# Third-FFN first chunk split in two parts, and the experts'-end operands moved out of the weight ring

## The chip, the cores and the metric

One core of one Trainium2 chip runs the kernel. The metric is device time in microseconds (us) of one execution. TensorE (PE) multiplies, ScalarE (ACT) and VectorE (DVE) work on tiles, SyncE (SP) issues the transfers; GpSimd (POOL) has nothing to do here.

## What is computed

A transformer block with a mixture of experts and then two layers of a second block, for 256 tokens of width 1024, all in float32. Each of the two layers is FFN, token mixer, FFN, every one of them behind an adaptive norm whose gain, shift and gate come from a product of a condition vector with a large matrix `w_ada`. The parts that the change touches:

```python
def ada_norm(x, g, shift, scale):
    return rms_norm_2(x, g) * (1 + scale[:, None, :]) + shift[:, None, :]

def swiglu(h, w13, w2):
    a, b = jnp.split(h @ w13, 2, axis=-1)
    return (jax.nn.silu(a) * b) @ w2
...
x = first_block(x, ...)            # ends with the experts
for l in range(2):
    h = ada_norm(x, norm_g[l, 0], mod[:, 0, 0], mod[:, 0, 1])
    x = x + 0.5 * mod[:, 0, 2][:, None, :] * swiglu(h, ffn_w13[l, 0], ffn_w2[l, 0])
    ...                            # token mixer, then a second FFN
```

So there are four FFNs: first (layer 0, right behind the experts), second, third (layer 1, right behind the second), fourth.

## The kernel before

**Tiles and products.** The stream `XT` lies transposed, 8 chunks of 128 features by 256 tokens. Weights come from HBM in pieces of 1 MB (128 rows of 2048 floats). A piece lands in a tile of the ring `raw` and is split for PE into a rounded part `hi` and the rest `lo` (`split`, lines 316 and 320): ACT copies 128x1024 to `hi`, DVE subtracts twice 128x512 for `lo`, two such halves to a piece. PE then makes a product of three float32r terms (hi x hi, hi x lo, lo x hi: lines 340 and 342). A product of plain float32 operands needs no split; PE runs it in two passes.

**An FFN's start.** The norm's factor r (one number per token) needs the whole stream. So the first chunk (j = 0) of `w13` is multiplied with x times g, which needs no r: `early` writes x times g into `self.xg` (with two columns of the shift behind the 256 tokens), chunk by chunk as the stream gets ready; `ff_early` (line 617) multiplies it with piece 0 in float32; `ff_joined` applies r afterwards. Meanwhile `rstd` makes r, and `normalize` (lines 533, 378, 379) makes `hl`, the normalized hi and lo, from which the chunks j = 1 to 21 are multiplied (`ff_in`). `xg` and piece 0 both lie in tiles of the ring `raw`. At the end of the experts `xg` is written by DVE (line 544), elsewhere by ACT (line 546).

**Rings.** `rings(raw, split)` closes the three pools `raw`, `hi`, `lo` and opens them anew with other numbers of buffers. The experts run with (6, 3), the FFNs with (4, 5). In the kernel before, `moe_end` switches them, and `ffn` calls it behind `ff_early` and `rstd`. The tiles of a new pool may be written once the old pools that lay in the same place are done with. The same `moe_end` closes the experts' pools `moe0` and `moe1`, opens the ring `ada_pool(2)` for `w_ada` (tiles `araw`), and loads some constants.

**Where the pools lie.** In a partition of SBUF, in bytes: `moe0` from 72,320, `moe1` from 118,240 to 152,608, in it the tile `xl` (the low part of the gathered rows, read by the first-round experts) from 123,840 to 140,224; the first FFN's pool (`hT`, `acc`) from 73,632 to 126,880; the two `araw` tiles behind the experts from 138,976 to 155,360; the (6, 3) rings from 155,232, the (4, 5) rings from 155,360 up to the same end, 229,344; in both the ring `raw` has the upper end.

**Order.** Each engine's order is made when the program is built, by a planner that takes, of the instructions whose inputs its own model holds to be ready, the one that stands first in the code. DVE's subtractions of the second to the sixth half piece behind an FFN's last chunk are tied behind that chunk's square (`HOLD`, `add_sq`, line 462). An `ada` step multiplies one araw tile: the first step behind the experts by eight PE products (line 1089), the steps inside an FFN by four DVE operations (lines 1117 and 1119).

Of the kernel before, what the change touches and what calls it, by code (L numbers as in the profile page):

```python
# [10 lines left out]
F32 = mybir.dt.float32  # L11
F32R = mybir.dt.float32r
# [3 lines left out]
AF = mybir.ActivationFunctionType  # L16
OP = mybir.AluOpType
# [3 lines left out]
P = 128  # L21
S = 256
D = 1024
NC = 8
# [8 lines left out]
RINGS = (4, 5)  # L33
# [191 lines left out]
class Net:  # L225
# [269 lines left out]
    def after(self, ins, prev):  # L495
        self.tc.add_manual_dep(ins.ins, prev.ins.name, mybir.DependencyInfo(
            mybir.DependencyClass.NoSync, mybir.DependencyReason.DATA), reason="activation table")
# [35 lines left out]
            nc.vector.scalar_tensor_tensor(h, self.XT[:, c, :], gs[:, c:c + 1], r, OP.mult, OP.mult)  # L533
            self.put_hl(hl, c, h, None if shift is None else shift[:, c:c + 1])

    def early(self, gs, shift, m, dve=False):

        nc = self.nc
        if m == 0:
            self.xg = self.raw()[:, 0:NC * 258].rearrange("p (a c) -> p a c", a=NC)  # L540
            nc.vector.tensor_copy(self.xg[:, :, 256:258], shift[:, :, None].to_broadcast([P, NC, 2]))
        out, x, g = self.xg[:, m, 0:256], self.XT[:, m, :], gs[:, m:m + 1]
        if dve:
            nc.vector.tensor_scalar(out, x, g, None, OP.mult)
        else:
            nc.scalar.activation(out, x, AF.Copy, scale=g)

    def newton(self, x, n):

# [31 lines left out]
    def out_proj(self, dram, hl, gate=None, after=None, early=None):  # L581
        for j in range(4):
            one = j == 3
            for a, ps in enumerate(self.pair(dram[j], hl, "x", one)):
                m = 2 * j + a
                self.resid(ps, m, gate, one)
                after(m) if after else self.add_sq(m, 2)
                if early:
                    early(m)
# [15 lines left out]
            nc.vector.tensor_tensor(s, s, tb, OP.mult)  # L605
        self.put_hl(hT, j, s)

    def ff_early(self, dram):

        nc = self.nc  # L610
        pss = [self.ps("x"), self.ps("x")]
        raw = self.raw()
        nc.sync.dma_start(raw[:, 0:2048], dram)
        for k in range(NC):
            for a, ps in enumerate(pss):
                o = 256 * k + a * P
                nc.tensor.matmul(ps[:, 0:258], raw[:, o:o + P], self.xg[:, k, :], start=(k == 0), stop=(k == NC - 1))  # L617
        return pss
# [12 lines left out]
    def ff_out(self, hT, dram, gate, after, gs=None):  # L631
        h = NFF // 2
        for m in range(NC):
            ps = self.ps("x")
            one = m == NC - 1
            for a in range(2):
                self.mm_t([ps], self.piece(dram[2 * m + a], h, P), P, P, hT, a * h, a == 0, a == 1, one)
            if one:
                self.ada_flush()
            self.resid(ps, m, gate, one)  # L640
            self.add_sq(m)
            if gs is not None:
                self.early(*gs, m)
            if not one:
                after(m)


    def first_block(self):
        nc = self.nc
        self.table("natural_log_exp_and_others")  # L650

        hl = self.hl()
        g = self.v("mix_g", 0, 8)
        for c in range(NC):
            x = self.XT[:, c, :]
            nc.scalar.activation(hl[:, c, 0, :], x, AF.Copy, scale=g[:, c:c + 1])
            nc.vector.scalar_tensor_tensor(hl[:, c, 1, :], x, g[:, c:c + 1], hl[:, c, 0, :].bitcast(F32), OP.mult, OP.subtract)  # L657
        self.mark("norm1")
        self.ada_pool(2)
        es, T = self.phase("mix1")  # L660
        mix = self.mixer1(hl, T)
        self.table("natural_log_exp_and_others")
        es.close()
        self.m1_es.close()
        self.mark("ada0")
        self.ada(ADA1[0])
        self.mark("out1")
        self.ada_pool(4)
        es, T = self.phase("moe0")
        moe = Moe(self, T)  # L670
        self.out_proj(self.ap["w1o"], mix, after=moe.token_rows)
        self.mark("ada0")
        self.ada(ADA1[1])
        self.ada_pool()
        self.rings(6, 3)
        es2, moe.T = self.phase("moe1")
        moe.run()

        def end():
            es2.close()  # L680
            es.close()
            self.rings(*RINGS)
            self.ada_pool(2)
            self.second_consts()
        self.moe_end = end
# [485 lines left out]
    def ffn(self, l, f, sub, gate, n0, n1, n2, ph=None, nxt=None):  # L1171

        self.mark(f"ffi{l}{f}")
        assert self.ada_at >= 40 * l + (8, 32)[f]
        first = self.ff_early(self.ap[f"w13_{l}{f}"][0])
        r = self.rstd(self.nps[:, :256], 1.0 / D)
        if l == f == 0:
            self.moe_end()
        self.ada(n0)
        es, hT, acc = ph or self.ffn_phase(l, f, n1 + n2)  # L1180
        hl = self.hl()
        self.table("silu_and_others")
        self.normalize(hl, r, *sub)
        self.ff_joined(hT, first, r)
        for j in range(NFF):
            if j:
                self.ff_in(hT, j, self.ap[f"w13_{l}{f}"][j], hl)
            self.ada((j + 1) * n1 // NFF - j * n1 // NFF, acc)
        self.table("natural_log_exp_and_others")
        assert self.ada_at >= (40 * l + 16, 48 if l == 0 else 80)[f]  # L1190
        self.mark(f"ffo{l}{f}")
        self.ff_out(hT, self.ap[f"w2_{l}{f}"], gate, lambda m: self.ada((m + 1) * n2 // 7 - m * n2 // 7, acc), nxt)
        es.close()
# [383 lines left out]
class Moe:  # L1577
# [312 lines left out]
    def run(self):  # L1890
        net, nc, T = self.net, self.net.nc, self.T
# [11 lines left out]
        net.tc.no_sync_barrier()  # L1903
        net.mark("gather")

        xs = (net.t(net.hl_p, [P, NC, 512], F32R, "hl"), T([P, NC, 512], "xl", 1, F32R))
        for c in range(NC):
            for src, dst in zip((hh, hw), xs):
                pg = net.ps("x")
                for t in range(2):  # L1910
                    nc.tensor.matmul(pg, src[:, t, c * P:(c + 1) * P], Pm[:, t, 0:512], start=(t == 0), stop=(t == 1))
                if c % 2 or dst is xs[0]:
                    nc.scalar.activation(dst[:, c, :], pg, AF.Copy)
                else:
                    nc.vector.tensor_copy(dst[:, c, :], pg)
        for t in range(2):
            nc.vector.tensor_tensor(Pm[:, t, 512:].rearrange("p (c n) -> p c n", n=64),
                                    self.iota[:, None, :64].to_broadcast([P, 12, 64]),
# [2 lines left out]
        gs = self.slot_gates(lambda t, g: Pm[:, t, g * P:(g + 1) * P].bitcast(F32), self.TILES)  # L1921
# [14 lines left out]

        net.mark("moe")

        def after(m):
            net.sum_sq(m)  # L1940
            for e in range(2):
                net.early(net.gs[0][:, 0:8], net.mod[0][:, 0:8], m + e, True)


        n = len(self.WORK)
        x, yos = {}, [self.T0([P, 2, 4, 256], "m8", 4, F32R) for _ in range(2)]
        pgs, ys = {}, {}
        for i in range(n + 2):
            if i < n:
                g = self.WORK[i]  # L1950
                r, es = self.TILES[g]
                if r and r not in x:
                    x[r] = gathered(r)
                if r == 0:
                    sl = slice(g * P, (g + 1) * P)
                    pgs[g] = self.split_in(g, lambda c: xs[0][:, c, sl], lambda c: xs[1][:, c, sl])
                else:
                    o = (g % 2) * P
                    pgs[g] = self.whole_in(r, es, lambda c: x[r][:, c, o:o + P])
            if i >= 2:  # L1960
                g = self.WORK[i - 2]
                PT = self.tokens(lambda t: Pm[:, t, g * P:(g + 1) * P])
                if i == n + 1:
                    net.table("natural_log_exp_and_others")
                    net.mark("scat")
                self.scatter(ys.pop(g), PT, "aa" if i < n + 1 else "ddaa", None if i < n + 1 else after)
            if 1 <= i <= n:
                g = self.WORK[i - 1]
                r, es = self.TILES[g]
                y = self.whole_out(r, es, pgs.pop(g), gs[:, g]) if r else self.split_out(g, pgs.pop(g), gs[:, g])  # L1970
                ys[g] = self.rows_out(y, yos[i % 2])
# [64 lines left out]
```

## Time and profile before

| | |
|---|---|
| Median of 3 runs | 1429.32 us (1427.37 to 1429.59) |
| The profiled execution | 1427.89 us, its span 1426.1 us |
| Granted TensorE clock, mean over the span | 0.989 |
| Busy share | PE 96%, DVE 74%, ACT 54% |
| HBM read | 324 MB, 228 GB/s over the span |

Matmul records overlap, so PE's busy share says whether it was waiting, not how well it ran. The kernel's time is the span plus 1.8 us around it.

### The profile page before, as it was taken

Reading aid. Unit: us, or ns where it says so; the run is one execution under the profiler, and the core shown is the slowest. Engines: PE = TensorE matmul, PEld = TensorE weight load, DVE = VectorE, ACT = ScalarE, POOL = GpSimd, SP = SyncE. Lnnn points to the kernel's source line nnn. Section 1 sums busy time; section 2 is a strip of 40 time slices with the busy share of each in tenths; the row PEclk is TensorE's granted clock in tenths of the full one; section 3 lists DMA queues with packets and bytes.
Section 4 is the critical chain, followed back from the end, with each engine's and each line's share of the span. In section 5 each row is a group of like instructions: output and inputs, shape, how many; then the busy total and the mean of one; then the engine's idle time right before and its main releaser. Section 6 shows DMA issues by size and latency. Waiting matters only on the chain.

```text
span 1426.1 us, 21863 instructions
## 1 busy us (share of the span) xinstructions
PE 1369.0 (96%) x8054; PEld 1093.7 (77%) x8059; DVE 1052.3 (74%) x2412; ACT 770.8 (54%) x1483; POOL 0.2 (0%) x4
## 2 busy tenths in 40 slices
PE   7998899998999999898999999999999998999997
PEld 6756575545888888566888888888888676888886
DVE  8997645537988557676999876798688586877664
ACT  7555434324665544544766556565555455766553
POOL 0000000000000000000000000000000000000000
PEclk9999899999999999999999999999999999999999
DMA  8744578885886558632688575887487623455452
GB/s 311 285 162 172 238 269 337 337 330 225 334 318 230 171 170 308 239 131 89 213 306 307 179 265 180 330 310 267 155 300 284 247 94 115 156 202 197 142 180 71
DMA packets 51391, 326.49 MB, mean 229 GB/s; under 512 B 6209, under 2 KB 7378, under 8 KB 18898
## 3 DMA queue, kind: packets, MB, share of 16 engines
q1 hardware_dynamic: 50994, 324.86, 62.0%
q8 instruction: 64, 1.05, 0.3%
q14 instruction: 45, 0.37, 0.1%
q10 hardware_dynamic: 288, 0.20, 0.1%
HBM read 324.00 MB, written 1.05 MB: 228 GB/s over the span
## 4 chain that ended last, share of the span: by engine, by line
PE 88%; DVE 5%; ACT 3%; DMA 2%; issue 1%; SPq 0%; DVEq 0%; ACTq 0%
PE psd L340 13%; PE pse L340 12%; PE psa L340 10%; PE psd L342 7%; PE pse L342 6%; PE psa L342 6%; PE psd L356 3%; PE psd L358 3%; PE psd L357 3%; PE psd L1825 3%; PE psm L1089 2%; PE pse L1825 2%; PE psa L1881 1%; DVE lo L320 1%; PE psd L617 1%
## 5 line engine op out<-in xcount | busy, mean ns | idle before, releaser
L320 DVE TENSOR_TENSOR lo<-raw,hi 128x512 fp32r<-128x512 f32 x832 | 503.6, 628 | 175.9 <-ACT hi L316 174.9
L316 ACT ACTIVATE hi<-raw 128x1024 fp32r<-128x1024 f32 (+3 forms) x418 | 400.6, 962 | 339.3 <-PE pse L340 82.0
L340 PE MATMUL psd<-hl,hi 128*128 128x512 f32 x592 | 213.5, 401 | 9.3 <-DVE hl L657 6.8
L340 PE MATMUL pse<-hl,hi 128*128 128x512 f32 x496 | 177.0, 398 | 5.4 <-ACT hi L316 5.4
L342 PE MATMUL psd<-hl,lo 128*128 128x256 f32 x640 | 180.2, 283 | 0.0
L340 PE MATMUL psa<-hl,hi 128*128 128x512 f32 x464 | 164.3, 395 | 0.8 <-ACT hi L316 0.6
L342 PE MATMUL pse<-hl,lo 128*128 128x256 f32 x512 | 144.0, 281 | 0.0
L342 PE MATMUL psa<-hl,lo 128*128 128x256 f32 x512 | 143.7, 281 | 0.0
L340 PEld LDWEIGHTS psd<-hl,hi 128*128 128x128 f32 x592 | 111.5, 189 | 38.7 <-ACT hi L316 8.6
L342 PEld LDWEIGHTS psd<-hl,lo 128*128 128x128 f32 x640 | 121.8, 190 | 1.2 <-DVE lo L320 0.7
L340 PEld LDWEIGHTS pse<-hl,hi 128*128 128x128 f32 x496 | 93.7, 189 | 29.8 <-ACT hi L316 6.3
L340 PEld LDWEIGHTS psa<-hl,hi 128*128 128x128 f32 x464 | 86.9, 188 | 21.0 <-ACT hi L316 0.9
L342 PEld LDWEIGHTS pse<-hl,lo 128*128 128x128 f32 x512 | 97.3, 190 | 0.5 <-DVE lo L320 0.4
L342 PEld LDWEIGHTS psa<-hl,lo 128*128 128x128 f32 x512 | 96.7, 189 | 0.9 <-DVE lo L320 0.4
L1119 DVE SCALAR_TENSOR_TENSOR acc<-araw,cact,acc 128x512 f32<-128x512 f32 x118 | 85.5, 745 | 0.1
L356 PE MATMUL psd<-hi,hl 128*128 128x512 f32 (+3 forms) x224 | 84.6, 378 | 0.8 <-ACT hl L378 0.4
L357 PE MATMUL psd<-lo,hl 128*128 128x512 f32 (+3 forms) x224 | 83.7, 374 | 0.0
L358 PE MATMUL psd<-hi,hl 128*128 128x512 f32 (+3 forms) x224 | 83.1, 373 | 0.0
L340 PE MATMUL pse<-hT,hi 128*128 128x512 f32 x220 | 78.2, 398 | 0.0
L340 PE MATMUL psd<-hT,hi 128*128 128x512 f32 x220 | 78.0, 397 | 0.0
L342 PE MATMUL pse<-hT,lo 128*128 128x256 f32 x264 | 74.3, 281 | 0.0
L342 PE MATMUL psd<-hT,lo 128*128 128x256 f32 x264 | 74.2, 281 | 0.0
(565 smaller groups left out, 2425.5 us busy)
## 6 DMA issues: line engine op xcount, KB each, us to landing
raw<-w SPq DMA_DIRECT2D x88, 1024.0 KB, 5.0
araw<-wada SPq DMA_DIRECT2D x64, 1024.0 KB, 6.9
raw<-w SPq DMA_DIRECT2D x64, 704.0 KB, 4.1
raw<-egu SPq DMA_DIRECT2D x32, 1024.0 KB, 7.2
raw<-edn SPq DMA_DIRECT2D x16, 1024.0 KB, 6.7
raw<-w2n SPq DMA_DIRECT2D x12, 1024.0 KB, 6.4
raw<-cw SPq DMA_DIRECT2D x8, 1024.0 KB, 6.4
araw<-wadb SPq DMA_DIRECT2D x8, 1024.0 KB, 6.0
```

The lines of the kernel that those rows point to most:

```text
L316: nc.scalar.activation(hi[:, f:g], src[:, f:g], AF.Copy)
L320: ins = nc.vector.tensor_tensor(lo[:, f:g], src[:, f:g], hi[:, f:g].bitcast(F32), OP.subtract)
L340: nc.tensor.matmul(ps[:M, :].rearrange("p (a b) -> p a b", a=2), hi[:, o:o + M], xhl[:, k0 + k, :, :], start=st, stop=False)
L342: nc.tensor.matmul(ps[:M, 0:256], lo[:, o:o + M], xhl[:, k0 + k, 0, :], start=False, stop=sp)
L356: nc.tensor.matmul(o, xh, wh, start=st, stop=False)
L357: nc.tensor.matmul(o, xh, wl, start=False, stop=False)
L358: nc.tensor.matmul(o, xl, wh, start=False, stop=sp)
L617: nc.tensor.matmul(ps[:, 0:258], raw[:, o:o + P], self.xg[:, k, :], start=(k == 0), stop=(k == NC - 1))
L1089: self.together(4, lambda j: self.nc.tensor.matmul(self.ada_acc[32 * j:32 * j + 32, :n], lhsT, rhs[:, n * j:n * j + n], start=start, stop= ...
L1119: nc.vector.scalar_tensor_tensor(acc[:, w], raw[:, w], self.cact[:, c, 0:1], acc[:, w], OP.mult, OP.add)
L1825: self.net.halves(lambda h: nc.tensor.matmul(out[p(h)], lhsT[:, p(h)], rhs(h), start=start, stop=stop, tile_position=(0, 64 * h)))
L1881: nc.tensor.matmul(ps[:, 256 * e:256 * e + 256], y[:, i, m0 + k, e * P:(e + 1) * P], PT, start=(e == 0 and i == 0), stop=(i == 1), skip_gr ...
```

## The change

Two places change.

1. **Behind the experts (first FFN).** `xg` and piece 0 no longer lie in the ring `raw`: both lie in one tile `last` of pool `moe1`, with the tag `xl` (the tag grows by 64 bytes, and `hl` by 128, so that `xl` begins at 123,968 and ends at 140,416; piece 0 is its upper half). The switch of the rings to (4, 5) moves from `moe_end`, behind `ff_early`, to right behind `moe.run()`. The rest of `moe_end` stays where it was. `early` still writes with DVE there.
2. **Third FFN.** `xg` is now a tile of pool `hl`, in two parts (hi by ACT, lo by DVE, per chunk of the second FFN's end). Piece 0 is split like all others, `ff_early` makes three float32r products of 258 columns for each float32 one, and `normalize` writes `hl` into the same tile over `xg`.

The second and the fourth FFN keep the float32 form in the ring `raw`.

```diff
-    def early(self, gs, shift, m, dve=False):
+    def early(self, gs, shift, m, xg=None):
         nc = self.nc
+        x, g = self.XT[:, m, :], gs[:, m:m + 1]
+        sh = shift[:, :, None].to_broadcast([P, NC, 2])
+        if xg == "split":
+            if m == 0:
+                self.xg = self.t(self.hl_p, [P, NC, 2, 258], F32R, "hl")
+                hi = self.xg[:, :, 0, 256:258]
+                nc.scalar.activation(hi, sh, AF.Copy)
+                nc.vector.tensor_tensor(self.xg[:, :, 1, 256:258], sh, hi.bitcast(F32), OP.subtract)
+            hi, lo = (self.xg[:, m, i, 0:256] for i in range(2))
+            nc.scalar.activation(hi, x, AF.Copy, scale=g)
+            nc.vector.scalar_tensor_tensor(lo, x, g, hi.bitcast(F32), OP.mult, OP.subtract)
+            return
         if m == 0:
-            self.xg = self.raw()[:, 0:NC * 258].rearrange("p (a c) -> p a c", a=NC)
+            self.xg = (self.raw() if xg is None else xg)[:, 0:NC * 258].rearrange("p (a c) -> p a c", a=NC)
...
-    def ff_early(self, dram):
+    def ff_early(self, dram, raw=None):
         pss = [self.ps("x"), self.ps("x")]
-        raw = self.raw()
+        if len(self.xg.shape) == 4:
+            pieces = self.piece(dram, NC, 256)
+            for ip, (hi, lo, ks) in enumerate(pieces):
+                for a, ps in enumerate(pss):
+                    for i, k in enumerate(ks):
+                        o = 256 * i + a * P
+                        for j, (w, x) in enumerate(((hi, 0), (hi, 1), (lo, 0))):
+                            nc.tensor.matmul(ps[:, 0:258], w[:, o:o + P], self.xg[:, k, x, :], start=(ip == i == j == 0),
+                                             stop=(ip == len(pieces) - 1 and i == len(ks) - 1 and j == 2))
+            return pss
+        if raw is None:
+            raw = self.raw()
         nc.sync.dma_start(raw[:, 0:2048], dram)
...
         es2, moe.T = self.phase("moe1")
         moe.run()
+        self.rings(*RINGS)
         def end():
             es2.close()
             es.close()
-            self.rings(*RINGS)
             self.ada_pool(2)
             self.second_consts()
...
-        first = self.ff_early(self.ap[f"w13_{l}{f}"][0])
+        first = self.ff_early(self.ap[f"w13_{l}{f}"][0], self.raw0 if l == f == 0 else None)
...
-        hl = self.hl()
+        hl = self.xg[:, :, :, 0:256] if len(self.xg.shape) == 4 else self.hl()
...
+        last = None
         def after(m):
+            nonlocal last
+            if m == 0:
+                last = T([P, NC * 514], "xl")
+                net.raw0 = last[:, NC * 258:]
             net.sum_sq(m)
             for e in range(2):
-                net.early(net.gs[0][:, 0:8], net.mod[0][:, 0:8], m + e, True)
+                net.early(net.gs[0][:, 0:8], net.mod[0][:, 0:8], m + e, last)
```

## Rows read from the trace of the kernel before

**Rows 1.** The page's chain that ended last: its shares by engine.

```profile
PE 88%; DVE 5%; ACT 3%; DMA 2%; issue 1%; SPq 0%; DVEq 0%; ACTq 0%
```

**Rows 2.** Timeline, PE, behind the experts: start us, us, engine line, operation, count, [idle before].

```profile
325.86 3.65 PE L1825 MATMUL pse<-raw,ehf 128*64 128x512 f32 x16
...
336.63 6.26 PE L617 MATMUL psd<-raw,raw 128*128 128x258 f32 x28
342.82 1.06 PE L1089 MATMUL psm<-araw,cact 128*32 128x512 f32 x8
349.29 0.80 PE L340 MATMUL pse<-hl,hi 128*128 128x512 f32 x1 [5.41 <-ACT hi L316]
...
352.77 0.39 PE L340 MATMUL pse<-hl,hi 128*128 128x512 f32 x1
...
353.12 0.39 PE L340 MATMUL pse<-hl,hi 128*128 128x512 f32 x1
```

**Rows 3.** The chain in order of time, same stretch: start us, us, what.

```profile
342.92 4.93 DMA raw<-w
...
348.18 1.06 ACT hi L316
```

**Rows 4.** Waits of the transfer queue (SP), 310 to 346 us: total, times, longest.

```profile
SPq L695 <- DVE m L1857: 13.9, 1, 13.9
SPq L300 <- PE psd L617: 7.0, 1, 7.0
```

**Rows 5.** Windows: busy us of PE, PEld, DVE, ACT, POOL; granted clock, DMA share, GB/s.

```profile
343.00:349.30 6.30, 0.89 (x9) 0.01 (x1) 4.68 (x15) 2.62 (x6) 0.00 (x0) 0.99 0.84 317
349.30:351.00 1.70, 1.70 (x4) 1.17 (x5) 1.70 (x3) 1.57 (x2) 0.00 (x0) 0.50 1.05 443
...
366.60:378.00 11.40, 11.40 (x68) 10.05 (x67) 11.32 (x23) 7.18 (x13) 0.00 (x0) 1.00 0.93 374
```

**Rows 6.** Timeline, PE, from the second FFN's end into the third.

```profile
873.44 0.28 PE L337 MATMUL pse<-hT,hi 128*128 128x256 f32 x1
...
873.67 0.28 PE L342 MATMUL pse<-hT,lo 128*128 128x256 f32 x1
...
882.91 7.13 PE L617 MATMUL psa<-raw,raw 128*128 128x258 f32 x32
889.97 1.92 PE L1089 MATMUL psm<-araw,cact 128*32 128x512 f32 x16
891.83 0.50 PE L340 MATMUL psd<-hl,hi 128*128 128x512 f32 x1
```

**Rows 7.** Timeline, DVE, from the second FFN's end into the third.

```profile
881.92 2.49 DVE L320 TENSOR_TENSOR lo<-raw,hi 128x512 fp32r<-128x512 f32 x4
884.33 1.27 DVE L533 SCALAR_TENSOR_TENSOR w<-XT,gs,w 128x256 f32<-128x256 f32 x3
...
891.51 0.41 DVE L626 TENSOR_TENSOR w<-psa,w 128x256 f32<-128x256 f32 x1
```

**Rows 8.** Timeline, DVE, behind the experts.

```profile
337.79 1.67 DVE L533 SCALAR_TENSOR_TENSOR w<-XT,gs,w 128x256 f32<-128x256 f32 x4 [2.41 <-ACT w L490]
...
339.71 1.67 DVE L379 SCALAR_TENSOR_TENSOR hl<-w,mod,hl 128x256 fp32r<-128x256 f32 x4
...
344.86 0.48 DVE L379 SCALAR_TENSOR_TENSOR hl<-w,mod,hl 128x256 fp32r<-128x256 f32 x1
```

**Rows 9.** Timeline, SP, behind the experts: the issues in their order.

```profile
332.03 0.34 SPq L695 DMA_DIRECT2D k_cmask<-k_cmask  x1
...
335.38 0.43 SPq L1106 DMA_DIRECT2D araw<-wada  x1
...
342.92 2.12 SPq L300 DMA_DIRECT2D raw<-w  x4
```

**Rows 10.** The tile araw, 300 to 420 us: from issue to landing, us.

```profile
DMA to landing us min/median/max: 5.2/7.0/11.0
```

**Rows 11.** PE's products of line 1089, whole span: idle before them, us, times.

```profile
  DMA araw<-wada: 2.1, 2
```

More of the change, by code (lines that the diff above doesn't have):

```diff
@@ L534, in normalize @@
             self.put_hl(hl, c, h, None if shift is None else shift[:, c:c + 1])
-    def early(self, gs, shift, m, dve=False):
+    def early(self, gs, shift, m, xg=None):
         nc = self.nc
-        if m == 0:
-            self.xg = self.raw()[:, 0:NC * 258].rearrange("p (a c) -> p a c", a=NC)
-            nc.vector.tensor_copy(self.xg[:, :, 256:258], shift[:, :, None].to_broadcast([P, NC, 2]))
-        out, x, g = self.xg[:, m, 0:256], self.XT[:, m, :], gs[:, m:m + 1]
-        if dve:
+        x, g = self.XT[:, m, :], gs[:, m:m + 1]
[10 more added lines that the diff above has]
+            return
+        if m == 0:
+            self.xg = (self.raw() if xg is None else xg)[:, 0:NC * 258].rearrange("p (a c) -> p a c", a=NC)
+            nc.vector.tensor_copy(self.xg[:, :, 256:258], sh)
+        out = self.xg[:, m, 0:256]
+        if xg is None:
+            nc.scalar.activation(out, x, AF.Copy, scale=g)
+        else:
             nc.vector.tensor_scalar(out, x, g, None, OP.mult)
-        else:
-            nc.scalar.activation(out, x, AF.Copy, scale=g)
     def newton(self, x, n):
@@ L642, in ff_out @@
             if gs is not None:
-                self.early(*gs, m)
+                self.early(*gs, m, "split")
             if not one:
@@ L1904, in run @@
         net.mark("gather")
-        xs = (net.t(net.hl_p, [P, NC, 512], F32R, "hl"), T([P, NC, 512], "xl", 1, F32R))
+        xs = (net.t(net.hl_p, [P, NC, 512], F32R, "hl"), T([P, NC, 514], "xl", 1, F32R))
         for c in range(NC):
@@ L1912, in run @@
                 if c % 2 or dst is xs[0]:
-                    nc.scalar.activation(dst[:, c, :], pg, AF.Copy)
+                    nc.scalar.activation(dst[:, c, 0:512], pg, AF.Copy)
                 else:
-                    nc.vector.tensor_copy(dst[:, c, :], pg)
+                    nc.vector.tensor_copy(dst[:, c, 0:512], pg)
         for t in range(2):
```

## The prediction

> **What bounds the kernel now.** I read the chain that ended last first. PE holds 88% of it [rows 1], so a change counts where PE stands idle or where its products get fewer. The change touches two places, and PE looks different in each.
>
> Behind the experts PE does stand idle. Its timeline [rows 2] shows the last expert product ending at 329.51 us, piece 0's float32 products ending at 342.89, eight ada products until 343.88, and then nothing for 5.41 us until piece 1's first product at 349.29. The chain in order of time says why [rows 3]: a transfer of 4.93 us that is issued at 342.92, then ACT's copy to hi. The queue's waits say why it is issued so late [rows 4]: the load of piece 1 waits for PE's line 617, which is piece 0's products, because x times g and piece 0 lie in the old ring `raw`, and the new rings can be filled only when the old ones are done with. The windows add a second price [rows 5]: behind the gap the granted clock is 0.50, that is 1.2 GHz, and back at 1.00 later. The five steps from 349.29 to 352.77 take 3.48 us; at the 0.35 us of the next step (352.77 to 353.12) they would take 1.75. So the gap costs 5.41 + 1.73 = 7.14 us.
>
> Into the third FFN PE never waits [rows 6]: product follows product until piece 1 begins at 891.83. There DVE is the engine that is full, from 881.92 to 891.92 [rows 7].
>
> **The change behind the experts.** With x times g and piece 0 in `last`, the last reader of the old ring `raw` is the last expert product, at 329.51. The four loads that now go out at 342.92 can go out from 329.5, 13.4 us earlier. Piece 1 then lands at 329.5 + 4.93 = 334.4 [rows 3]; ACT's first copy (1.06) gives hi at 335.5, or at about 336.1 if the two squares of the stream's last chunks go first; a first DVE subtraction (2.49 / 4 = 0.62, [rows 7]) gives lo before 337. PE wants it at 342.9. So the gap of 7.14 us goes. What hides the transfer and the split is PE's own work until 342.9 (scatter, sums of squares, piece 0); without that cover they would cost their 6.6 us (4.93 + 1.06 + 0.62) and the slow clock again.
>
> What the change adds here. Piece 1's four subtractions, 2.49 us, now fall between 336 and 338.6, beside DVE's idle time of 2.41 us that ends at 337.79 [rows 8]; `normalize` is late by some 0.8 us. In the kernel before it ended at 345.34 [rows 8], when PE had nothing to do anyway. Now PE starts at 342.9 and wants one chunk of `hl` each 0.35 us; the first four were done by 341.4 [rows 8] and will be by 342.2, the last by 346.1, wanted at 346.8. Behind that DVE still has `ff_joined` (six operations, some 2 us by those of like shape, [rows 7, 8]), and then piece 2's subtractions, wanted by PE from 348.5. DVE is busy 11.32 of 11.40 us somewhat later [rows 5], so it has no spare time to catch up quickly: PE may run in step with DVE for two or three chunks. No row shows this lag. Below it is 0; above it is 3.1 us, which is what PE loses when piece 1's subtractions come behind all of `normalize` (345.34 + 0.62 = 346.0 against 342.9). I take 1.0, nearer to 0, since the times above all fit by 0.3 us or more.
>
> The constants' loads, k_cmask and those behind it, stay where they were, since `moe0` is done with at the same moment as before [rows 9]. The load of the first `araw` does not. Its ring lies over `moe1`, and `moe1` now holds `last`, read by PE until 342.9; so both araw loads, of which the second went out at 335.38 [rows 9], now go out from 342.9. Their work (1.06 us of PE, four DVE operations) is only moved, if it is taken when it is there. This is where the change can turn on itself; it is a rival below.
>
> Piece 0's own load costs nothing: `xl` is free once the last first-round expert is multiplied, and the load has until piece 0's products. The chunks of x times g are written by the same DVE operations as before.
>
> Sum of this part: -7.14 + 1.0 = -6.1 us.
>
> By the Trainium skill (TensorE: Matmul & The Clock Gate, section HAM oscillation — how this bites in real kernels), a wait for data between two bursts of products can send TensorE back to half rate for the start of the second burst. This trace agrees, with 0.50 behind a gap of 5.41 us; by that rule a remaining gap of like length would keep the 1.73 us too.
>
> **The change in the third FFN.** Removed: 32 float32 passes of 258 columns, 7.06 us from 882.91 to 889.97 [rows 6]. Added: 48 float32r products of 258 columns. Those of 256 columns follow each other at (873.67 - 873.44) / 2 = 0.115 to 0.118 us [rows 6]; at 0.1185 for 258 it makes 5.69. PE saves 1.37 us.
>
> Added on ACT: two copies of 1.06 us; on DVE: four subtractions (2.49 us) and eight operations for the low part of x times g, 0.48 each by the like operation of line 379 [rows 8]. Most lie inside the second FFN's end, where PE sets the pace and both have idle time, so they cost nothing; without that cover they would cost 6.3 us of DVE. Not all: piece 0 now counts in `HOLD`, so its second half and both halves of piece 1 are tied behind the last square. In the DVE row the four subtractions from 881.92 to 884.33 were of pieces 1 and 2 [rows 7]; now two are piece 0's, then comes the last low part (0.48), and piece 1's first half fits partly before r is there. `normalize`, which now writes over x times g chunk by chunk behind PE, starts some 0.6 us later. PE comes to piece 1 at 891.83 - 1.37 = 890.5. Its first four chunks are then ready (about 890); piece 1's second half, wanted at 893.3, comes at about 893.4. Bounds: 0, or 3.8 us if piece 1's first half comes behind `normalize` and `ff_joined` (891.92 + 1.72 + 0.62 = 894.3 against 890.5). I take 0.4. Sum: -1.37 + 0.4 = -1.0 us.
>
> The freed buffer of `raw` lets loads run further ahead; PE waits for none there, so it is worth nothing.
>
> **Sum.** -6.1 - 1.0 = -7.1 us on the profiled execution's 1427.89: 1420.8. The median of the runs is 1.43 us above that execution, so 1422.2.
>
> **The rivals.** A run to run spread of 2.2 us makes 0.2% (2.9 us) about what can be told.
>
> Lag: one of the two DVE bounds comes true. Behind the experts: piece 1 at 346.0, -7.14 + 3.1 = -4.0, with the third FFN's -1.0: 1424.3. In the third FFN: +2.4 instead of -1.0: 1425.6. For it speaks a full DVE in both places; against it that the planner put four subtractions ahead of `normalize` at the third FFN as soon as DVE was free [rows 7].
>
> Late araw, the other side: PE's order keeps the eight ada products right behind piece 0, as now [rows 2]. Then PE waits for an araw issued at 342.9, which takes 5.2 to 11.0 us, 7.0 in the middle [rows 10]: products at 349.9, piece 1 at 351.0 instead of 349.29, +1.7 and -1.0 for the third FFN, 1430.0; at 11.0 it is +5.7, 1434.0. It is slower than before from a landing time of 6.3 us on, and by over 0.2% from 9.2. For it: it is the code's order. Against it: SP's order shows that what is not ready is passed over (the second araw goes out ahead of the loads of pieces 1 and 2, which the code has ahead of it, [rows 9]), and in the whole run PE waited for an araw only twice, 2.1 us in all [rows 11].
>
> Blocked queue: the araw loads stand ahead of the pieces on SP, as they do now [rows 9]; then the pieces wait with them until 342.9, the gap stays, and only the third FFN's -1.0 and 0.4 of an extra issue remain: 1428.7. Against it: at 329.5 the pieces are ready and the araw are not. The Trainium skill (DMA: Bandwidth & Descriptors, section Anatomy of one DMA — SWDGE (gpsimd) path) has every semaphore wait of a transfer happen on the issuing engine ahead of dispatch, so one waiting issue holds all behind it. The trace agrees: a constant's load held SP for 13.9 us [rows 4].
>
> **How the numbers follow.** The forecast has 0.48, lag 0.23 (half in each place), blocked queue 0.12, late araw 0.17, of which 0.06 within 0.2% and 0.11 above. Faster: 0.48 + 0.23 = 0.71; same: 0.12 + 0.06 = 0.18; slower: 0.11. The forecast's own range is 1419.7 (both lags 0: -8.5, so 1420.8, less half of the spread) to 1424. The range goes from 1419.7 to 1429.0: it leaves out the slower 0.11 and a little on either side.
>
> **What would show it.** The four loads of pieces 1 to 4 at about 329.5, ahead of both araw; no gap of PE behind piece 0 and no clock of 0.50 there; the eight ada products inside piece 1 or 2; piece 1 at about 343; in the third FFN 48 products in 5.7 us and piece 1 about 1.4 us after them plus the 1.9 of ada. A PE wait on araw, or a DVE that is late for pieces 1 and 2, would make it wrong.

## The result, and the profile after

| | before | after |
|---|---|---|
| median (lowest to highest), us | 1429.45 (1427.37 to 1429.64), 4 runs | 1418.80 (1417.88 to 1420.97), 4 runs |
| profiled execution: time, span | 1427.89, 1426.1 | 1419.36, 1417.6 |

The ratio is 0.9929, 95% interval 0.9913 to 0.9944: 10.65 us less by the medians, 8.5 us by the two spans. The forecast was 1422.2, its range 1419.7 to 1429.0. The direction was right, the forecast gain was too small, and the result lies 0.9 us below the range.

PE behind the experts, the timeline of the changed kernel (start us, us, engine, line, operation, count); it answers to [rows 2]:

```profile
338.85 5.82 PE L641 MATMUL psd<-xl 128*128 128x258 f32 x26
344.32 0.58 PE L340 MATMUL pse<-hl,hi 128*128 128x512 f32 x1
344.74 0.28 PE L342 MATMUL pse<-hl,lo 128*128 128x256 f32 x1
...
351.74 1.07 PE L1113 MATMUL psm<-araw,cact 128*32 128x512 f32 x8
```

Piece 1 follows piece 0 without a gap, and the eight ada products come 7 us behind the end of piece 0, between others. The windows (busy us of PE, PEld, DVE, ACT, POOL; granted clock, DMA share, GB/s) have no half clock there, where [rows 5] had 0.50:

```profile
343.00:345.00 2.00, 2.00 (x11) 1.76 (x10) 1.74 (x5) 1.88 (x2) 0.00 (x0) 1.00 0.92 389
345.00:347.00 2.00, 2.00 (x14) 1.72 (x13) 2.00 (x7) 1.69 (x5) 0.00 (x0) 1.00 0.63 176
347.00:349.00 2.00, 2.00 (x13) 1.56 (x12) 2.00 (x7) 1.83 (x4) 0.00 (x0) 1.00 1.04 438
```

The queue's issues, the timeline of SP in the same stretch, against [rows 9]:

```profile
331.15 0.34 SPq L300 DMA_DIRECT2D raw<-w  x1
...
334.89 0.43 SPq L300 DMA_DIRECT2D raw<-w  x1
335.42 0.37 SPq L714 DMA_DIRECT2D w<-k_sel  x1
335.83 2.65 SPq L300 DMA_DIRECT2D raw<-w  x2
344.70 0.81 SPq L1130 DMA_DIRECT2D araw<-wada  x2
```

Piece 1's load leaves when the last expert product ends (327.46 + 3.65 = 331.1 us here). The other three pieces leave by 338.5, and both araw last, at the end of piece 0. That is the order that the prediction gave, but for the three pieces behind the constants. On DVE (its timeline) piece 1's four subtractions come ahead of `normalize`, as foreseen; there is even a wait of 0.95 us for k_sel, and PE waits for none of it:

```profile
337.34 1.29 DVE L320 TENSOR_TENSOR lo<-raw,hi 128x512 fp32r<-128x512 f32 x2 [0.37 <-ACT hi L316]
338.81 1.29 DVE L320 TENSOR_TENSOR lo<-raw,hi 128x512 fp32r<-128x512 f32 x2 [0.17 <-ACT hi L316]
340.02 1.67 DVE L533 SCALAR_TENSOR_TENSOR w<-XT,gs,w 128x256 f32<-128x256 f32 x4
...
343.26 0.43 DVE L716 CAST k_selb<-w 128x512 bf16<-128x512 f32 x1 [0.95 <-DMA w<-k_sel]
```

PE in the third FFN, against [rows 6]:

```profile
876.08 0.59 PE L632 MATMUL psa<-hl,hi 128*128 128x258 f32 x2
...
881.87 0.28 PE L632 MATMUL psa<-hl,lo 128*128 128x258 f32 x1
882.08 1.93 PE L1113 MATMUL psm<-araw,cact 128*32 128x512 f32 x16
883.93 0.50 PE L340 MATMUL psd<-hl,hi 128*128 128x512 f32 x1
```

From the first product of piece 0 to the first ada product it is 6.00 us; it was 889.97 - 882.91 = 7.06 [rows 6]. Between them the 48 products need 0.125 us each, where the prediction took 0.1185.

**Where the 8.5 us are.** The two gains of the prediction, 7.1 and 1.0, would make 8.1, but they are not all that differs. The span was cut at the first and last product of piece 0 and of each output stage (the products that read hT), by PE's rows, so each length is a difference of two starts (read to 0.01 us, then rounded). Lengths in us:

```
                                       before   after   difference
piece 0 of FFN 1                          8.5     8.7     +0.2
input stage of FFN 1 (gap in it)        126.9   120.1     -6.8
output stage of FFN 1                    62.1    61.4     -0.7
mixer of layer 0                        159.8   158.2     -1.6  (one stretch of half clock less)
input stage of FFN 2                    119.9   121.1     +1.2
output stage of FFN 2                    62.1    61.4     -0.7
from there through piece 0 of FFN 3       8.9     7.8     -1.2
input stage of FFN 3                    122.7   121.9     -0.8
output stage of FFN 3                    63.7    63.3     -0.4
mixer of layer 1                        153.2   154.4     +1.2  (one stretch of half clock more)
input stage of FFN 4                    116.9   116.9      0.0
output stage of FFN 4                    62.1    61.4     -0.7
from piece 0 of FFN 1 to the last       1082.2  1072.2   -10.0
```

(Piece 0 of the second and of the fourth FFN keep their 7.6 and 8.0 us.) So -10.0 us from the experts' end on, and +1.6 ahead of it, where the change adds no work. The windows behind the routing show where that comes from, of before first and then of after:

```profile
184.00:186.00 2.00, 2.00 (x7) 1.58 (x7) 0.56 (x4) 1.06 (x1) 0.00 (x0) 0.68 0.00 0
186.00:188.00 2.00, 2.00 (x11) 1.60 (x10) 1.62 (x3) 1.13 (x2) 0.00 (x0) 1.00 0.00 0
```

```profile
184.00:186.00 2.00, 2.00 (x6) 1.52 (x6) 0.92 (x6) 0.67 (x1) 0.00 (x0) 0.50 0.00 0
186.00:188.00 2.00, 2.00 (x6) 1.55 (x5) 1.29 (x2) 0.50 (x2) 0.00 (x0) 0.50 0.00 0
```

The granted clock stays at 0.50 for some 3.4 us longer in the changed kernel's execution, which costs half of that, 1.7 us. In the changed kernel's second profile (e4, below) half clock ends there as early as in before's, and e7, which has before's instructions in before's order, has the 3.4 us more, so this belongs to the execution and not to the change. With the gap's own 1.73 us apart, half clock inside the 1082.2 and the 1072.2 us is worth 5.1 us in both. So -10.0 us is the change, and the medians agree with it (-10.65).

What neither gain explains are the output stages, -2.4 us together, and the input stages of FFN 2 and 3. There the instructions are the same, PE waits for nothing, and the products themselves run at another pace.

### The profile page after: what moved, and what is told of

Read it like the earlier page. It is cut to its first block, busy times and chain, and to the rows that moved or that the text cites. A ratio compares the mean times of both kernels' runs of the same rounds, so it can differ in the third digit from the quotient of the medians.

```text
span 1417.6 us, 21913 instructions
## 1 busy us (share of the span) xinstructions
PE 1365.7 (96%) x8070; PEld 1093.5 (77%) x8075; DVE 1056.5 (75%) x2424; ACT 771.6 (54%) x1486; POOL 0.2 (0%) x4
## 4 chain that ended last, share of the span: by engine, by line
PE 89%; DVE 5%; ACT 3%; DMA 2%; issue 1%; SPq 0%; DVEq 0%; ACTq 0%
PE psd L340 13%; PE pse L340 12%; PE psa L340 11%; PE psd L342 7%; PE pse L342 6%; PE psa L342 6%; PE psd L356 3%; PE psd L358 3%; PE psd L357 3%; PE psd L1849 3%; PE psm L1113 2%; PE pse L1849 2%; PE psa L1905 1%; PE psd L641 1%; PE pse L1526 1%
```

## Experiments

Each kernel ran beside the kernel before on one chip; edits are shown against the changed kernel, and for e3 and e7 against the kernel before. Where executions differ by their stretches of half clock, the stages' lengths are compared; those of the kernel before come from its one profile.

**The two halves of the change, a tile moved, and the change again.** Theory 1: both gains are as computed with hardly any lag, and a third one comes from the place of hT: the ring of `hl` is 128 bytes a partition wider for the two times 258 columns, and all tiles behind it, hT too, lie 128 bytes further. Rival: the prediction's lags are real, and the pace differs from execution to execution.

The experts' end alone (e1):

```
-                self.early(*gs, m, "split")
+                self.early(*gs, m)
```

> Only the experts' end is changed (buffer of the experts' rows for x times g and piece 0, rings filled early); the third FFN keeps its 32 float32 passes and no tile grows. Theory 1, the sum of the prediction with its lag at nothing: the gap of 5.41 us and the 1.73 us of half clock go and nothing is paid back, -7.1 us. Rival, the prediction as it stood with a lag of 1.0: -6.1 us, with a wait of PE on DVE in pieces 1 and 2. The FFNs' output products keep the 397 ns that they have in the kernel before, since hT lies where it lay.

1422.34 us against 1432.19, ratio 0.9925 (0.9902 to 0.9948). The input stage of FFN 1 takes 119.9 us for 126.9: -7.0, with no wait of PE on DVE there, so the lag is 0.1 us at most. The output stages keep 62.1 and 63.7 us. But two input stages change as well: FFN 3's takes 120.9 us for 122.7, and FFN 4's 119.2 for 116.9. From FFN 2 on this kernel has each engine's instructions in before's order, PE's operands lie at the same addresses, and PE waits for nothing in either. Rows of FFN 3 from 925 us on, of before and of e1:

```profile
L340 PE MATMUL psd<-hl,hi x43: 395/398/403, 927.4 to 964.9; 128*128 128x512 f32 x43
```

```profile
L340 PE MATMUL psd<-hl,hi x42: 391/391/391, 924.9 to 961.3; 128*128 128x512 f32 x42
```

The third FFN alone (e2):

```
-        self.rings(*RINGS)            (behind moe.run(); the xl tiles are 512 wide again)
+            self.rings(*RINGS)        (in end(), as before)
-                last = T([P, NC * 514], "xl")
-                net.raw0 = last[:, NC * 258:]
+                last = net.raw()
+                net.raw0 = None
```

> Only the third FFN is changed (x times g in two parts, 48 products); the experts' end is that of the kernel before. The ring of hl is 128 bytes wider for it, so hT lies 128 bytes further. Theory 1: the 48 products save 1.1 us, and the products on hT run at 392 ns for 397, which gives 0.6 us in each of four FFNs, so -3.5 us in all. Rival, the prediction as it stood: -1.0 us, and what the products on hT take has to do with the execution and not with the place of hT.

1427.04 us against 1432.19, ratio 0.996 (0.9942 to 0.9979). The gap is there (126.9 us). From the output stage of FFN 2 through piece 0 of FFN 3 it takes 7.8 us for 8.9, and the four output stages take 61.4, 61.4, 63.3 and 61.4. From piece 0 of FFN 1 on that makes -3.1 us at equal clock, near theory 1's -3.5.

The kernel before with the wider ring alone (e3):

```
-        raw = net.t(net.hl_p, [P, 2, 2048], F32, "hl")
+        raw = net.t(net.hl_p, [P, 2, 2064], F32, "hl")[:, :, 0:2048]
```

> The kernel before with one thing changed: the ring of hl is made 128 bytes wider and the width isn't used. Each engine has the same instructions in the same order; all that lies behind hl (x, work tiles, hT) lies 128 bytes further. Theory 1, the place of hT sets the pace of the products that read it: 392 ns for 397 in all four FFN output stages, -2.4 us. Rival, it is a matter of the execution: within 0.5 us of the kernel before and 397 ns in some stages.

1429.34 us against 1432.19, ratio 0.9975 (0.996 to 0.999). The output stages take 61.4, 61.4, 63.4 and 61.4 us: -2.3 in all, by nothing but a wider ring. The rival falls here, since e1 and e3 were profiled on the same chip and e1 kept the old lengths. The input stages move as well, in both directions: 128.2 for 126.9, 121.4 for 119.9, 120.9 for 122.7.

The changed kernel again, twice (e4, and later g2):

> The changed kernel as it is, once more, for a second profile and more times. Theory 1, half clock stretches of 3.4 us come and go between executions at 1.7 us each: this profile has another number of them behind the routing and in the second mixers, and the median lies 10 to 11 us below the kernel before; the pace of the products on hT is again 392 ns. Rival: the stretches stand where they stood in the first profile, and the difference is 8.5 us.

> The changed kernel as it is, beside the kernel with both places at multiples of 512 bytes, so that both are timed on one chip. Theory: 9 to 11 us below the kernel before by medians; the stages' lengths are those of its first two profiles within 0.3 us, and half clock stretches differ in number.

1419.42 us against 1432.19 (ratio 0.9897, 0.9874 to 0.9921) and 1420.16 against 1430.77 (0.9915, 0.9899 to 0.9931), so -12.8 us by medians, more than the 10 to 11 expected, and -10.6, within the 9 to 11. On the first of these chips, where e1 to e4 ran, the kernel before took 1426.9 to 1438.0 us, and the differences by medians from e1 to e4 are all 1.3 to 3.1 us larger than those by stages; no profile shows why, and the stages are what is used here. They have the lengths of the first profile within 0.3 us, but for the mixers (FFN 1's takes 119.8 us for 120.1), and the pace of each stage is the same each time. Half clock inside the stages is worth 6.8 us in both, against 5.1 in the first profile: it comes and goes by about 1.7.

**Is it hT's place, or that of a tile beside it?** The kernel before with hT alone 128 bytes on (e7):

```
-        hT = T([P, NFF, 2, 256], "hT", 1, F32R)
+        hT = T([P, NFF * 512 + 32], "hT", 1, F32R)[:, 32:].rearrange("p (k a c) -> p k a c", k=NFF, a=2)
```

> The kernel before with hT alone moved by 128 bytes, in a tile that is 128 bytes wider; hl, x and the work tiles stay where they are, and all instructions and their order are the same. Theory 1, it is the place of hT that sets the pace of the products reading it: the four output stages take 61.4, 61.4, 63.3 and 61.4 us in place of 62.0, 62.0, 63.6 and 62.1. Rival, it is the place of another tile (x or the work tiles): they keep the lengths of the kernel before. How fast the FFN input products run (391 or 398 ns) isn't foretold by either.

The rows of the second FFN's products on hT (ns min/median/max, first to last start), of before, of after and of this kernel:

```profile
L340 PE MATMUL psa<-hT,hi x44: 397/397/398, 834.2 to 849.4; 128*128 128x512 f32 x44
L342 PE MATMUL psa<-hT,lo x44: 281/281/281, 834.5 to 849.6; 128*128 128x256 f32 x44
```

```profile
L340 PE MATMUL psa<-hT,hi x44: 391/392/397, 828.1 to 843.1; 128*128 128x512 f32 x44
L342 PE MATMUL psa<-hT,lo x44: 278/280/283, 828.3 to 843.3; 128*128 128x256 f32 x44
```

```profile
L340 PE MATMUL psa<-hT,hi x44: 392/392/396, 836.4 to 851.4; 128*128 128x512 f32 x44
L342 PE MATMUL psa<-hT,lo x44: 278/280/283, 836.6 to 851.6; 128*128 128x256 f32 x44
```

44 products from first to last take 15.2 us in the first and 15.0 in the others. Three of the four output stages take 61.4 us as expected; the third takes 63.7, as in the kernel before, and misses the 63.3. So moving hT alone changes the pace in three of them. In the third it isn't enough: there e3, which moves x and the work tiles as well, has 63.4. The execution took 1428.59 us (one time).

The changed kernel with hT and its neighbours a further 128 bytes on (f1), by the same edit as e3 with 2080:

> The changed kernel with the ring of hl 128 bytes wider again, so hT and all behind hl lie 256 bytes further than in the kernel before; instructions and order are those of the changed kernel. If hT's pace follows its place in steps, the four output stages differ from 61.4, 61.4, 63.3 and 61.4 us again (62.0 if 256 bytes bring the old pace back); if only the old place was a bad one, they stay at 61.4. The input stages' pace (391 to 398 ns) may change too; which way, neither theory says.

62.1, 62.1, 63.7 and 62.1 us: the old pace is back. One time, 1420.23 us.

The changed kernel with `hl` and all behind it 32 bytes on, at a multiple of 512 bytes (f3):

```
-        self.cact = self.kp.tile([P, 8, 32], F32, name="cact32")
+        self.cact = self.kp.tile([P, 264], F32, name="cact32")[:, 0:256].rearrange("p (a b) -> p a b", a=8)
```

> The changed kernel with hl and all behind it moved on by 32 bytes, so that hl begins at a multiple of 512 bytes; instructions and order are those of the changed kernel. If the products on hl have a pace set by hl's place, all four input stages change together, by up to 1.8 us each (391 for 398 ns); if hl's place is not what sets it, they differ stage by stage as before. The output stages show hT at 160 bytes further than in the kernel before.

Rows of the input stage's products, FFN 2, from 735 us on: of before, of after, of e3 and of f3.

```profile
L340 PE MATMUL pse<-hl,hi x45: 391/391/391, 734.7 to 772.1; 128*128 128x512 f32 x45
```

```profile
L340 PE MATMUL psd<-hl,hi x42: 395/398/404, 737.7 to 774.8; 128*128 128x512 f32 x42
```

```profile
L340 PE MATMUL pse<-hl,hi x42: 395/398/403, 734.9 to 772.0; 128*128 128x512 f32 x42
```

```profile
L340 PE MATMUL psa<-hl,hi x48: 390/390/391, 734.7 to 773.2; 128*128 128x512 f32 x48
```

`hl` lies at one address in the first three, and yet the pace is 391 in one and 398 in the others. In the fourth it is 390 in FFN 1, 2 and 4, and FFN 2's input stage takes 119.4 us for 121.1. In FFN 3, where `hl` has 258 columns a part, it stays at 396. If `hl`'s place set their pace, the four were expected to change together. They don't: FFN 2's changes by 1.7 us, those of the others by 0.2 or less against e4. The output stages, with hT 160 bytes from its old place, take 61.7, 61.7, 63.3 and 61.7 us. One time, 1420.82 us.

**Which part of the change at the experts' end does it.** The rings' switch back in its old place (e5, the first two lines of e2's edit):

> The changed kernel with the switch to the new rings back in its old place, behind piece 0's products in the code; x times g and piece 0 stay in the experts' buffer. Theory 1, what frees the ring is that piece 0 and x times g no longer lie in it, and the order of the transfers follows the data and not the lines: piece 1 is loaded at about 331 us as in the changed kernel and PE has no gap. Rival, the place of the switch matters: piece 1 is loaded only when piece 0 is multiplied, at 344.7, and the gap of 5.4 us with its 1.7 us of half clock is back.

119.8 us in FFN 1's input stage, no gap, and the transfers are in the changed kernel's order. The planner makes the changed kernel's own program of it: each engine has the same instructions in the same order, at the same addresses. So the moved switch is no part of the gain, and this is a fourth profile of the changed kernel: piece 1's load is free as soon as nothing that PE still reads lies in `raw`. 1420.57 us (one time).

The eight ada products forced ahead of piece 1 (e6):

```
+        self.behind = self.ada_end if l == f == 0 else None      (behind self.ada(n0))
+                    if self.behind is not None:                  (at the next FFN input product)
+                        self.after(ins, self.behind)
+                        self.behind = None
```

> The changed kernel with one order forced: piece 1's first product comes behind the eight ada products, as it does in the kernel before. The prediction's rival of the late araw: araw is issued when piece 0 is multiplied, at about 344.7, and lands 5.2 to 11.0 us later, so PE stands still from 344.7 to about 350 to 351, with half clock behind it; stages behind that are 6 to 8 us later than in the changed kernel (1.7 us of it by the clock). Against it: if araw is issued earlier in this order, PE loses under 2 us.

Its PE timeline:

```profile
343.11 0.82 PE L341 MATMUL psa<-hl,hi 128*128 128x512 f32 x2
346.27 1.23 PE L341 MATMUL psd<-hl,hi 128*128 128x512 f32 x2 [2.34 <-DVE ffb L653]
...
351.90 1.06 PE L1117 MATMUL psm<-araw,cact 128*32 128x512 f32 x8
352.90 0.50 PE L341 MATMUL pse<-hl,hi 128*128 128x512 f32 x1
```

The ada products run 8.4 us after araw's issue at 343.50, as late as foretold. But PE doesn't stand still for them: the planner takes products into `psa` and `psd`, which are pieces 2 and 3, ahead of piece 1 (`pse`), and the wait that is left, 2.34 us, is for DVE to empty a `psd`. FFN 1's input stage takes 124.2 us for 120.1, +4.1 where 6 to 8 were expected (+4.5 against the 119.8 of e4, e5 and g2): 2.3 of waiting and 1.7 of half clock behind it (the windows from 346 to 350 have 0.62 and 0.52). By the Trainium skill (TensorE: Matmul & The Clock Gate, section HAM oscillation — how this bites in real kernels) a wait between bursts can bring half rate to the next burst; this profile agrees, with half clock behind 2.34 us as in before's behind the 5.41 of [rows 2]. 1421.96 us (one time).

**Versions that might be faster.** Piece 0 of the second and fourth FFN in two parts as well, with x times g in rows of hT that are written last (e8):

```
-            self.out_proj(..., early=lambda m: self.early(*sub(2), m))
+            self.out_proj(..., early=lambda m: self.early(*sub(2), m, ph[1]))
+                    self.xg = xg[:, 13:].rearrange("p k a c -> p (k a c)")[:, 0:NC * 516].rearrange(
+                        "p (k a c) -> p k a c", k=NC, a=2)
```

> The changed kernel with piece 0 of the second and the fourth FFN in two parts as well; x times g for it lies in the rows of hT that are written last. Theory 1: piece 0 takes 5.8 us for 6.8 (as the third FFN shows) in place of 7.6 to 8.0 with what is mixed into it, about 1 us less in each, -2 us against the changed kernel at equal clock. Rival: DVE, which also has the eight low parts and four subtractions more in each of the two, is late for piece 1, and 0 to 3 us come back.

1424.19 us (1422.37 to 1426.93) against 1429.85, ratio 0.9963 (0.9949 to 0.9977): slower than the change, which on this chip took 1420.57 (e5, one time). PE's waits around the fourth FFN's piece 0 (total, times, longest):

```profile
PE psa L340 <- ACT hl L378: 1.8, 1, 1.8
PE psd L340 <- DVE hl L379: 1.1, 1, 1.1
PE psd L342 <- DVE lo L320: 0.8, 1, 0.8
```

Piece 0 takes 7.0 us there for 8.0, but 3.7 us come back as waits, more than the rival allowed, and the input stage takes 123.0 us for 116.9: the waits, 1.7 us of half clock behind them, and 0.7 more. In the second FFN the mixer's end, piece 0 and the input stage together change by +0.4 us at equal clock. The likely reason, not tried by itself: in the third FFN ACT and DVE split x times g under an output stage that PE alone fills; these two have only the output projection ahead of them.

Both tiles at a multiple of 512 bytes (g1), f3's edit and hT's like e7's with 112 for 32:

> The changed kernel with hl moved on by 32 bytes and hT, within a wider tile, to the next multiple of 512 bytes; instructions and order are those of the changed kernel. Theory: as the start of hl at a multiple of 512 gave 390 ns in the input stages, hT's start there gives 390 ns in the output stages, 61.2 us or a little less in place of 61.4; with the 1.7 us that hl gave in the second FFN the kernel is 2 to 3 us below the changed kernel at equal clock. Rival: 61.4 or more in the output stages, and no more than 1.5 us below.

1414.18 us (1413.59 to 1415.91) against 1430.77, ratio 0.9882 (0.9864 to 0.9900), on the chip where the changed kernel had 1420.16. The row that answers to those of hT above:

```profile
L340 PE MATMUL psa<-hT,hi x44: 390/390/390, 825.3 to 840.2; 128*128 128x512 f32 x44
L342 PE MATMUL psa<-hT,lo x44: 282/282/282, 825.6 to 840.5; 128*128 128x256 f32 x44
```

The output stages take 61.0, 61.0, 62.6 and 61.0 us and FFN 2's input stage 119.4. From piece 0 of FFN 1 to the last product on hT it is 1067.2 us for the changed kernel's 1072.2, and with the half clock inside taken off (3.4 us here, 5.1 there) 1063.8 for 1067.1: 3.3 us less, and 2.6 to 3.7 against the changed kernel's other profiles, where 2 to 3 were expected. It is faster than both kernels, with the changed one's instructions in the same order; the 6.0 us between the two medians are more than the pace explains, and in these two profiles (g1 and g2) half clock makes another 3.4.

## Why the prediction was off

**Behind the experts: right in mechanism, its lag too large.** The transfer goes out at the end of the last expert product and the 7.14 us go. The lag of 1.0 us was measured at 0.1 (e1, -7.0) to 0.4 (after, -6.8), and at nothing in e4, e5 and g2 (-7.1). The estimate assumed that a DVE which is full must be late; here it had its subtractions done in the order that PE wanted, and still waited 0.95 us for a constant.

**The third FFN: right within 0.2 us at piece 0, but not paid in full.** -1.2 us against -1.0. The saving of 1.37 came out at 1.06, since 48 products take 0.125 us each and not 0.1185, a pace that was carried over from 256 columns; the lag of 0.4 didn't show, for PE waits for nothing in the whole stage. What no term had: its input stage takes 121.8 to 122.0 us, at 396 ns, in every profile with the split, and 120.9 without it in e1 and e3 (391 ns), 122.7 in before and e7 (398 ns). Against e1, the split gives 1.2 us at piece 0 and its input stage is 1.0 longer; against before it is 0.8 shorter. That it is the 258 columns a part, which put each chunk at another place, fits this but wasn't tried by itself.

**The step that failed is the sum.** It counted the two edited places, wrote "-6.1 - 1.0 = -7.1 us", and put all other stages at no change. They changed by about -2.1 us: output stages -2.4, FFN 2's input stage +1.2, FFN 3's -0.8, the mixers -0.4 and piece 0 of FFN 1 +0.2. The cause of the largest, the output stages, is shown: two columns more in the low and high part made the `hl` ring 128 bytes wider, so all behind it moved, hT too. The wider ring alone turns the new pace on (e3, -2.3), a still wider one turns it off again (f1), and moving hT alone turns it on in three of the four stages (e7, -2.0). That is some 2.4 of the 2.9 us by which -7.1 missed the measured -10.0; the lag behind the experts is 0.6 of the rest. The change's own description had `hl`'s 128 bytes; the prediction gave them no price.

**The rivals.** Lag, blocked queue and late araw did not come. Late araw was also priced too high: forced, it costs 4.1 us against the changed kernel and not the 8.8 that its +1.7 against a kernel with the gap of 7.14 means, because other pieces' products fill most of the wait.

**The spread.** The difference of the two profiled spans, 8.5 us, understates the change by 1.6, because the changed kernel's profile has half clock for longer behind the routing. Whether the prediction's offset of 1.43 us from the profiled execution to the median is of that kind isn't shown: those runs left no trace.

**Left open.** Why the pace follows the place of a tile, and why the input stages differ at one address of `hl` (391 to 398 ns from stage to stage, the same in the four profiles of the changed kernel), isn't settled. Place alone can't be all of it: e1 leaves all that PE reads and writes from FFN 2 on where it was, and FFN 3's and 4's input stages change by -1.8 and +2.3 us. What differs there are two work tiles of DVE and ACT, which have changed places; that they do it was not tried. So the changes of the input stages (+1.2 and -0.8 above) have no shown cause. That in f3 and g1 the three plain input stages all run at 390 ns may come from `hl`'s place or from that of what lies behind it; the runs move both. How many stretches of half clock an execution has, and why, was not tried.

## What to carry to other kernels

When a tile grows, list what lies behind it in memory: a product that nobody edited can change its pace, and over hundreds of products that can outweigh a term that was worked out with care. Before a gain of under 1% is put down to a cause, cut both profiles at the same products into stages, set the stages at half clock apart, and look whether the untouched stages kept their lengths. The split paid where the engines that do it are idle under PE's work (the third FFN), and not where PE came to wait for them (the fourth).

## What the runs showed of the hardware

- The pace of float32r products changed with the place of the moving tile: pairs of 512 and 256 columns on hT took 62.1 us a stage (FFN 1, 2 and 4), 61.4 with hT 128 bytes on, 61.7 with 160, 62.1 with 256, and 61.0 with hT at a multiple of 512 bytes. Counted from the last multiple of 256 bytes, these places are 160, 32, 64, 160 and 0 (hT begins at byte 73,632 in the kernel before), so the time rises with the distance; five places don't make it a rule, and e7's third stage breaks it. The Trainium skill (SBUF — State Buffer, section Operand start alignment) asks that an operand start at a multiple of its element's size, and says that this is about legality, not speed. All places here keep to it, and they still differ by 1.1 us in 62.
- The same products, in the same order and with their operands at the same addresses, ran at 398 ns in FFN 3 of the kernel before and at 391 in e1's. PE waited for nothing in either.
- TensorE's half clock (granted 0.50) came in stretches that cost about 1.7 us or twice that, and that differed in number between executions of one program: 5.1, 6.8, 3.4 and 6.8 us inside the stages in the four profiles of the changed kernel (after, e4, e5, g2).
